# A hybrid decoder block on one core: pool order and alignment, and the order of loads at two stage borders

## The chip, the core and the metric

The kernel runs on one core of a Trainium2 chip. The metric is the device time of one execution in microseconds; the kernel before has a median of 2562.64 us over 3 runs (2560.47 to 2562.73). The profile is of one more execution, which took 2560.91 us.

## The reference

One decoder layer over 512 tokens of width 2048, all in float32, one batch, depth 1.

```
h   = RMSNorm(x)
[qA|kA|vA|qB|kB|vB|gA|gB] = h @ W_in              # 2048 x 8704
yA  = sliding-window attention (window 128, ALiBi, sinks; 16 query, 4 key heads of 64)
yB  = stick-breaking attention (16 heads of 64, strictly causal, no softmax)
x   = x + (sigmoid(gA) * (yA @ W_branch_a) + sigmoid(gB) * (yB @ W_branch_b)) @ W_out
x   = x + (silu(gate) * up) @ W_down,   [gate|up] = RMSNorm(x) @ W_ffn_in   # 5632 each
out = RMSNorm_final(x)
```

## The kernel before, in words

Every product is made at float32 accuracy from three matmuls: each operand is split into a high part and a low part, and high x high, high x low and low x high are summed in PSUM. A weight tile comes in through SP's queue as `raw`, ScalarE casts it to `whi` (L150), VectorE subtracts to get `wlo` (L151). `W.next()` hands these chunks out in the order of a plan and keeps up to three chunks ahead (`fill`, `split`).

The stages, in the order in which TensorE sees them (times from the trace):

1. 0 to about 850 us: input projection. `features` (L330 to L332) streams `fh`/`fl`, the split transposed activations, against stationary weights (128x512 matmuls); `tokens` (L346 to L348) has `fh`/`fl` stationary and streams 256 weight columns. Pieces of both attentions are queued with `later` and taken one at a time by `gap()` between products.
2. About 850 to 1040 us: gates and branch projections, `features` again, from about 890 us on with `yh`/`yl` as the streamed operand.
3. About 1040 to 1217 us: `rows` (L846 to L848), the product with W_out in four column blocks n, with `mh`/`ml` stationary. After each block the residual is added (L890), squares are summed (L854), the sum is stored to `x2_d`, and it is transposed and turned into forms (`turn_x1`, `make_forms`).
4. About 1217 to 2104 us: gate/up, 11 groups of 28 chunks. It is a seven-product block scheme (p1, p5, p6, p3, p7, p2, p4 in `ORDER`): the weight blocks are summed on VectorE (L224) and the activations enter as *forms*, seven tiles `fx` for each of 8 pairs of 128-wide slices. A chunk is 12 matmuls of 128x512 (`product`, L253 to L255): 6 with the form of an even pair stationary, 6 with that of an odd pair. Weight chunks are streamed.
5. About 2104 to 2546 us: the down projection in four parts of 3, 3, 3 and 2 quads, the same scheme twice for each part. The forms come back from DRAM through POOL's queue (`load_forms`, L999), and the block sums `x2` through SP's (L987). `into` (L1020) adds each finished product to `x2`. In the last part each token tile is squared, multiplied with the final gain and scaled (`finish`).

Memory. Left-hand pools: `cp` (constants), `wp` (raw, whi, wlo, three of each) and `tp` (47 general slots of 2 KB a partition: `yh`, `yl`, attention tiles, residual tiles, part of the forms). Right-hand pools grow down from byte 229,344 of a partition: first `ca` (constants of the attention, 10,240 bytes), below it `ep` (32 slots: `fh`, `fl`, later `mh`, `ml`). After stage 3 both are closed, and `fp` takes their place with `wx` (lowest), `fx` and `wz`. 229,344 is 32 past a multiple of 64; all sizes are multiples of 64, so each tile of `ca`, `ep` and `fp` starts 32 past a multiple of 64. In the built program each tile of `wp` and `tp` starts at a multiple of 64 (`raw` at 18,944, `tp` at 55,808). The right-hand tiles lie at 153,568 and above, the left-hand ones below 152,064.

Of the 8 pairs of gate/up forms, pairs 4 to 6 lie in `fp` (`form_slot`), the others in `tp`. Of the forms of a down part, even pairs lie in `fp`, odd ones in `tp`.

Order at the two borders. At the end of stage 3 the code adds the residual, flushes the queued pieces, transposes the last four slices, and only then closes `early` and opens `fp` (L903 on); a planned chunk of gate/up can't be loaded before `fp` exists, as its `wx` tile lies there. Then come the second norm's sum and four generators of forms (pairs 4 to 7): two forms of each at once, the other five in one piece each. At the end of stage 4 all 16 `x2` tiles take a slot and are issued on SP's queue; then `load_forms` takes the forms' slots. The last group's transposes and forms (`turn`, `forms`, stores to `form_d` at L973 through POOL's queue) are pieces that run during the first products of stage 5.

The slots of a pool are given out in program order, earliest released first, and an engine's instructions run in their order: an instruction that waits holds all that stand behind it on its engine or queue.

Of the kernel before, what the change touches and what calls it, by code (L numbers as in the profile page):

```python
# [45 lines left out]
def kernel(  # L46
# [64 lines left out]
    make_identity(nc, ident)  # L111
    ones = const("ones", P)
# [132 lines left out]
    def product(forms, banks, first, last):  # L245

        wh, wl, _ = W.next()
        for kk in range(2):
            a = forms[kk]
            for t in range(2):  # L250
# [7 lines left out]
    def group(nq, forms, after):  # L258
# [597 lines left out]
    def form_slot(p, name):  # L856
        if 4 <= p < 7:
            return fp.tile([P, T], F32R, tag="fx", name=uid("fx"), bufs=21)
        return slot("fx", F32R)

    def turn_x1(k, xr, tag):
# [15 lines left out]
        if k % 2 and k < KD // 2:  # L877
            forms_of(k // 2)
# [5 lines left out]
    for n in range(4):  # L884
# [3 lines left out]
        rows(KD, mh, ml, ob)  # L888
        for t in range(NT):
# [7 lines left out]
    while pieces:  # L897
        pieces.popleft()[1]()
# [4 lines left out]
    early.close()  # L903
    fp = ctx.enter_context(tc.tile_pool(name="fp", bufs=1, side="right", reuse_waits="tile"))
    inv2 = const("inv2", NT)
    nc.vector.tensor_reduce(out=inv2, in_=ss2.rearrange("p (t c) -> p t c", t=NT), axis=AX.X, op=ALU.add)
    rsqrt_mean(inv2, inv2, NT, [small(s, NT) for s in ("rv", "rr", "rq")])

    W.fill()
    late = [make_forms(xs2[2 * p], xs2[2 * p + 1], lambda name, p=p: form_slot(p, name)) for p in range(4, 8)]  # L910
# [73 lines left out]
    x2 = [[slot("x2") for _ in range(4)] for _ in range(NT)]  # L984
    for n in range(4):
        for t in range(NT):
            nc.sync.dma_start(out=x2[t][n], in_=x2_d[t][n])  # L987
    sst = const("sst", 4 * NT)
    gf = [None] * 4

    def load_forms(p0, np):
        res = [{} for _ in range(np)]
        for name in FORMS:
            for i in range(np):
# [4 lines left out]
                nc.gpsimd.dma_start(out=res[i][name], in_=form_d[p0 + i][name])  # L999
        return res  # L1000
# [13 lines left out]
    def down(nq, forms, n, last):  # L1014
        def into(half, col, op, done=False, end=False):
            def fn(b):
                for i in range(2):
# [23 lines left out]
            },  # L1041
        )
# [50 lines left out]
```

## Time and profile before

| | us |
|---|---|
| median of 3 runs | 2562.64 |
| profiled execution | 2560.91 |
| its span, first to last instruction | 2559.2 |
| TensorE matmul busy | 2512.7 (98%) |
| VectorE busy | 1981.0 (77%) |
| ScalarE busy | 1377.3 (54%) |
| GpSimd busy | 241.7 (9%) |
| moved by DMA | 407.99 MB, mean 159 GB/s |

Busy matmul time is a weak measure here: a matmul's record (about 0.39 us) overlaps the next one, which starts some 0.23 us later. So the pace is read from start to start in the timeline, and idle time from the note in brackets behind a row, which says how long the engine stood idle and what ended it.

### The profile page before, as it was taken

To read this page: it belongs to the slowest core of one execution; us is meant where nothing else is said; L and a number is where in the kernel's file an instruction comes from. 1 tells how busy PE (TensorE), PEld (TensorE's weight loads), DVE (VectorE), ACT (ScalarE), POOL (GpSimd) and SP (SyncE) were. 2 spreads that over 40 slices of the span, in tenths; PEclk is the share of its full clock that TensorE was granted. 3 is DMA by queue.
4 is the path that set the end of the run, shared out by engine and by line. 5 is a ranking of instruction groups with operands and counts; after the bars stand their busy time and mean duration, and the time that the engine had idled before them with its cause. 6 is when DMAs were issued, how large, how long until landed. Compare 5 with 4: busy or idle time off the path is not lost.

```text
span 2559.2 us, 33175 instructions
## 1 busy us (share of the span) xinstructions
PE 2512.7 (98%) x11529; PEld 2063.9 (81%) x11529; DVE 1981.0 (77%) x3457; ACT 1377.3 (54%) x2626; POOL 241.7 (9%) x465
## 2 busy tenths in 40 slices
PE   9999999999999999999899999999999999999998
PEld 8888878888887788888688888888888877888886
DVE  5688888888779644374888788887888877888888
ACT  6567777666657533364554555554555443333335
POOL 0000001111111000000010011100111122303000
PEclk9999999999999999999999999999999999999999
DMA  5232333333323644443456655556555689948552
GB/s 174 91 99 91 99 108 99 103 95 109 98 87 106 213 143 138 141 145 116 153 169 192 183 180 176 177 177 189 181 173 181 193 273 331 308 153 279 177 179 97
DMA packets 257319, 407.99 MB, mean 159 GB/s; under 512 B 16480, under 2 KB 103552, under 8 KB 257152
## 3 DMA queue, kind: packets, MB, share of 16 engines
q1 hardware_dynamic: 204400, 308.32, 38.7%
q0 software_dynamic: 45632, 84.96, 11.0%
q10 hardware_dynamic: 7120, 12.61, 1.3%
q8 instruction: 90, 1.47, 0.2%
q14 instruction: 77, 0.63, 0.1%
HBM read 344.48 MB, written 61.34 MB: 159 GB/s over the span
## 4 chain that ended last, share of the span: by engine, by line
PE 62%; issue 2%; DVE 1%; ACT 1%; DMA 1%; POOL 0%; ACTq 0%; POOLq 0%; DVEq 0%
PE mm L253 9%; PE mm L255 9%; PE mm L254 9%; PE at L253 7%; PE at L255 7%; PE at L254 7%; PE mm L331 3%; PE mm L330 3%; PE mm L332 3%; PE mm L848 1%; PE mm L847 1%; PE mm L846 1%; PE at L848 1%; PE at L847 1%; PE at L846 1%
## 5 line engine op out<-in xcount | busy, mean ns | idle before, releaser
L150 ACT CAST whi<-wx 128x1024 fp32r<-128x1024 f32 x264 | 277.3, 1051 | 331.4 <-PE mm L255 150.6
L254 PE MATMUL mm<-wlo,fx 128*128 128x512 f32 x1056 | 418.1, 396 | 0.2 <-DVE wlo L151 0.2
L255 PE MATMUL mm<-whi,fx 128*128 128x512 f32 x1056 | 417.0, 395 | 0.0
L151 DVE TENSOR_TENSOR wlo<-wx,whi 128x1024 fp32r<-128x1024 f32 x264 | 322.7, 1223 | 115.4 <-ACT whi L150 114.1
L151 DVE TENSOR_TENSOR wlo<-raw,whi 128x1024 fp32r<-128x1024 f32 (+1 forms) x201 | 244.1, 1215 | 191.6 <-ACT whi L150 189.6
L253 PE MATMUL mm<-whi,fx 128*128 128x512 f32 x1056 | 377.1, 397 | 13.3 <-ACT whi L150 9.5
L150 ACT CAST whi<-wz 128x1024 fp32r<-128x1024 f32 x198 | 208.0, 1050 | 288.4 <-PE mm L255 142.8
L332 PE MATMUL mm<-fh,wlo 128*128 128x512 f32 x896 | 356.0, 397 | 1.4 <-DVE wlo L151 1.4
L330 PE MATMUL mm<-fh,whi 128*128 128x512 f32 x896 | 355.7, 397 | 0.0
L331 PE MATMUL mm<-fl,whi 128*128 128x512 f32 x896 | 355.5, 397 | 0.0
L150 ACT CAST whi<-raw 128x1024 fp32r<-128x1024 f32 (+1 forms) x201 | 209.7, 1044 | 225.6 <-PE mm L331 142.1
L254 PE MATMUL at<-wlo,fx 128*128 128x512 f32 x792 | 311.6, 393 | 4.7 <-DVE wlo L151 4.7
L255 PE MATMUL at<-whi,fx 128*128 128x512 f32 x792 | 312.4, 394 | 0.0
L583 ACT COPY turned<-z 32x128 f32<-32x128 f32 (+3 forms) x888 | 242.5, 273 | 104.5 <-DVE z L743 57.6
L151 DVE TENSOR_TENSOR wlo<-wz,whi 128x1024 fp32r<-128x1024 f32 x198 | 240.6, 1222 | 53.6 <-ACT whi L150 53.4
L253 PE MATMUL at<-whi,fx 128*128 128x512 f32 x792 | 281.2, 395 | 0.5 <-ACT whi L150 0.5
L253 PEld LDWEIGHTS mm<-whi,fx 128*128 128x128 f32 x1056 | 198.6, 189 | 57.8 <-ACT whi L150 10.4
L254 PEld LDWEIGHTS mm<-wlo,fx 128*128 128x128 f32 x1056 | 199.9, 189 | 45.6 <-DVE wlo L151 1.3
L255 PEld LDWEIGHTS mm<-whi,fx 128*128 128x128 f32 x1056 | 199.7, 189 | 45.2
L332 PEld LDWEIGHTS mm<-fh,wlo 128*128 128x128 f32 x896 | 169.3, 189 | 42.9 <-DVE wlo L151 2.6
L331 PEld LDWEIGHTS mm<-fl,whi 128*128 128x128 f32 x896 | 169.3, 189 | 38.1
L330 PEld LDWEIGHTS mm<-fh,whi 128*128 128x128 f32 x896 | 169.4, 189 | 37.3
(252 smaller groups left out, 4166.5 us busy)
## 6 DMA issues: line engine op xcount, KB each, us to landing
raw<-in_w_in_dram SPq DMA_DIRECT2D x135, 512.0 KB, 3.6
raw<-in_w_ffn_in_dram SPq DMA_DIRECT2D x88, 512.0 KB, 3.7
wz<-in_w_ffn_in_dram SPq DMA_DIRECT2D x88, 512.0 KB, 4.4
wx<-in_w_ffn_in_dram SPq DMA_DIRECT2D x44, 512.0 KB, 4.5
raw<-in_w_ffn_down_dram SPq DMA_DIRECT2D x44, 512.0 KB, 4.8
wz<-in_w_ffn_down_dram SPq DMA_DIRECT2D x44, 512.0 KB, 5.4
raw<-in_w_out_dram SPq DMA_DIRECT2D x32, 512.0 KB, 3.7
wx<-in_w_ffn_down_dram SPq DMA_DIRECT2D x22, 512.0 KB, 4.8
```

The costliest lines, as they stand in the source:

```text
L150: nc.scalar.copy(hi[:, :n], raw[:, :n])
L151: nc.vector.tensor_tensor(out=lo[:, :n], in0=raw[:, :n], in1=f(hi[:, :n]), op=ALU.subtract)
L253: mm(banks[t], lhsT=hi, rhs=wh[:, kk, :], start=one, stop=False, skip_group_check=True)
L254: mm(banks[t], lhsT=hi, rhs=wl[:, kk, :], start=False, stop=False, skip_group_check=True)
L255: mm(banks[t], lhsT=lo, rhs=wh[:, kk, :], start=False, stop=end, skip_group_check=True)
L330: mm(b, lhsT=wh[:, kk, c], rhs=hi[k], start=(k == 0), stop=False)
L331: mm(b, lhsT=wh[:, kk, c], rhs=lo[k], start=False, stop=False)
L332: mm(b, lhsT=wl[:, kk, c], rhs=hi[k], start=False, stop=(k == nk - 1))
L583: copy(t4[c * Q : (c + 1) * Q, :, r], z4[r * Q : (r + 1) * Q, :, c])
L846: mm(banks[t], lhsT=hi[k][:, c], rhs=wh[:, kk, :], start=(k == 0), stop=False)
L847: mm(banks[t], lhsT=hi[k][:, c], rhs=wl[:, kk, :], start=False, stop=False)
L848: mm(banks[t], lhsT=lo[k][:, c], rhs=wh[:, kk, :], start=False, stop=(k == nk - 1))
```

## The change

- A pool `pad` of 24 floats (96 bytes) is opened first on the right-hand side, and `ep` is opened before `ca`. So `ep` starts under byte 229,248, a multiple of 64, and `ca` lies below it. One GpSimd memset writes the pad.
- Pieces are flushed, `early` is closed, `fp` is opened and `W.fill()` is called right behind the last block's matmuls, ahead of the residual additions. Forms of pair 4 are made with those of pairs 0 to 3, in `tp`; pairs 5 to 7 lie in `fp`. The late generators are three; after two forms of each at once, the next three are one form to a piece; the sum of the second norm is a piece behind them.
- The `x2` tiles go through POOL's queue, two token tiles at a time, in `load_forms` of the first part, ahead of the form whose product reads them first; those of columns n = 2, 3 come behind all forms.
- The last product p4 (two chunks) takes both chunks first and then runs by token tile: all matmuls of tile 0, its addition and `finish`, then tile 1.

```diff
     early = ctx.enter_context(ExitStack())
+    pad = ctx.enter_context(tc.tile_pool(name="pad", bufs=1, side="right"))
+    unused = pad.tile([P, 24], F32, tag="pad", name="pad")
+    ep = early.enter_context(tc.tile_pool(name="ep", bufs=32, side="right"))
     ca = early.enter_context(tc.tile_pool(name="ca", bufs=1, side="right"))
-    ep = early.enter_context(tc.tile_pool(name="ep", bufs=32, side="right"))
...
-    def product(forms, banks, first, last):
+    def product(forms, banks, first, last, chunk=None, tiles=(0, 1)):
-        wh, wl, _ = W.next()
+        wh, wl, _ = chunk or W.next()
...
+            if tail and name == "p4":
+                chunks = [W.next() for _ in range(nq)]
+                for t in range(2):
+                    for j in range(nq):
+                        product([forms[2 * j + i][name] for i in range(2)], u, False, j == nq - 1, chunks[j], (t,))
+                    after[name](u, (t,))
+                return
...
     def form_slot(p, name):
-        if 4 <= p < 7:
+        if p >= 5:
...
-        if k % 2 and k < KD // 2:
+        if k % 2 and k < KD // 2 + 2:
             forms_of(k // 2)
...
         rows(KD, mh, ml, ob)
+        if n == 3:
+            while pieces:
+                pieces.popleft()[1]()
+            early.close()
+            fp = ctx.enter_context(tc.tile_pool(name="fp", bufs=1, side="right", reuse_waits="tile"))
+            W.fill()
...
+    late = [make_forms(xs2[2 * p], xs2[2 * p + 1], lambda name, p=p: form_slot(p, name)) for p in (5, 6, 7)]
     for _ in range(2):
         for p, gen in enumerate(late):
-            xforms[4 + p] = next(gen)
+            xforms[5 + p] = next(gen)
+    for _ in range(3):
+        for gen in late:
+            later(lambda gen=gen: next(gen), 1)
     for gen in late:
         later(lambda gen=gen: [None for _ in gen], 1)
+    later(norm2, 1)
...
+    def load_x2(n, half):
+        for t in (2 * half, 2 * half + 1):
+            x2[t][n] = slot("x2")
+            nc.gpsimd.dma_start(out=x2[t][n], in_=x2_d[t][n])
+
+    FIRST_READ = {"p1": (0, 0), "p5": (1, 1), "p6": (1, 0), "p4": (0, 1)}
...
         for name in FORMS:
+            if p0 == 0 and name in FIRST_READ:
+                load_x2(*FIRST_READ[name])
```

## Rows read from the trace of the kernel before

**Rows 1.** The page: each engine's busy us, share of the span, instructions.

```profile
PE 2512.7 (98%) x11529; PEld 2063.9 (81%) x11529; DVE 1981.0 (77%) x3457; ACT 1377.3 (54%) x2626; POOL 241.7 (9%) x465
```

**Rows 2.** Busy us (instructions) of each engine in a stretch, clock, DMA share, GB/s.

```profile
2300.00:2400.00 100.00, 100.00 (x432) 80.84 (x431) 80.94 (x81) 37.65 (x37) 20.44 (x38) 1.00 0.76 236
```

**Rows 3.** TensorE's timeline: start us, length us; `fh` streamed, 25 starts apart.

```profile
250.01 0.40 PE L330 MATMUL mm<-fh,whi 128*128 128x512 f32 x1
...
255.84 0.40 PE L331 MATMUL mm<-fl,whi 128*128 128x512 f32 x1
```

**Rows 4.** TensorE's timeline, `yh` streamed, 27 starts apart.

```profile
1019.69 0.39 PE L332 MATMUL mm<-yh,wlo 128*128 128x512 f32 x1
...
1025.81 0.39 PE L332 MATMUL mm<-yh,wlo 128*128 128x512 f32 x1
```

**Rows 5.** TensorE's timeline in gate/up, p5: 16 starts with pairs 4 to 6, then 6 with pair 7.

```profile
1454.47 0.39 PE L254 MATMUL at<-wlo,fx 128*128 128x512 f32 x1
...
1458.20 0.40 PE L253 MATMUL at<-whi,fx 128*128 128x512 f32 x1
...
1459.59 0.62 PE L253 MATMUL mm<-whi,fx 128*128 128x512 f32 x2
```

**Rows 6.** TensorE's timeline, `mh`/`ml` stationary, 17 starts apart.

```profile
1213.29 0.39 PE L846 MATMUL at<-whi,mh 128*128 128x512 f32 x1
...
1217.25 0.39 PE L848 MATMUL at<-whi,ml 128*128 128x512 f32 x1
```

**Rows 7.** TensorE's timeline at the border to gate/up; in brackets idle us, who ended it.

```profile
1217.48 1.93 PE L107 MATMUL at<-ident,x 128*128 128x128 f32 x16
1224.83 1.22 PE L253 MATMUL mm<-whi,fx 128*128 128x512 f32 x2 [5.42 <-ACT whi L150]
...
1247.89 0.68 PE L254 MATMUL at<-wlo,fx 128*128 128x512 f32 x1 [3.32 <-DVE wlo L151]
```

**Rows 8.** Busy time by stretch around that border (columns as in rows 2).

```profile
1217.25:1251.64 34.39, 24.04 (x90) 17.75 (x88) 32.04 (x66) 22.95 (x50) 1.62 (x3) 0.85 0.64 214
1231.00:1248.00 17.00, 12.28 (x51) 8.83 (x51) 17.00 (x32) 9.26 (x18) 0.00 (x0) 1.00 0.41 126
1205.00:1215.00 10.00, 10.00 (x45) 8.03 (x44) 0.00 (x0) 0.00 (x0) 0.00 (x0) 1.00 0.12 45
```

**Rows 9.** SP's queue at that border: start us, length us, DMAs issued.

```profile
1217.44 2.54 SPq L217 DMA_DIRECT2D wx<-in_w_ffn_in_dram  x4
```

**Rows 10.** VectorE's timeline there: a chunk's low part, and two low parts of forms.

```profile
1246.62 1.22 DVE L151 TENSOR_TENSOR wlo<-wx,whi 128x1024 fp32r<-128x1024 f32 x1
...
1248.09 0.75 DVE L279 TENSOR_TENSOR fx<-turned,fx 128x256 fp32r<-128x256 f32 x2
```

**Rows 11.** TensorE's timeline at the border from gate/up to down.

```profile
2109.22 0.79 PE L253 MATMUL mm<-whi,fx 128*128 128x512 f32 x1 [3.79 <-DMA fx<-f1p]
...
2137.87 0.73 PE L253 MATMUL mm<-whi,fx 128*128 128x512 f32 x2 [4.05 <-ACT whi L150]
```

**Rows 12.** Busy time by stretch before and at that border (columns as in rows 2).

```profile
2105.16:2142.55 37.39, 29.03 (x111) 22.54 (x111) 23.99 (x36) 14.52 (x25) 13.50 (x26) 0.86 1.06 347
2030.00:2100.00 70.00, 70.00 (x311) 57.13 (x310) 57.54 (x69) 36.39 (x51) 17.61 (x33) 1.00 0.84 254
```

**Rows 13.** Timelines of POOL's queue, SP's queue and ScalarE at that border.

```profile
2102.64 0.54 POOL L999 DMA_DIRECT2D fx<-f1p  x1
...
2101.42 16.54 SPq L987 DMA_DIRECT2D x<-x  x16
...
2136.29 0.58 ACT L965 COPY e<-at 128x512 f32<-128x512 f32 x1 [8.14 <-DMA f20p<-fo]
```

**Rows 14.** The end: TensorE's last matmul, and ScalarE's last four scalings.

```profile
2546.33 0.40 PE L255 MATMUL mm<-whi,fx 128*128 128x512 f32 x1
...
2550.81 2.56 ACT L1009 ACTIVATE x<-x,inv 128x512 f32<-128x512 f32 x4 [0.69 <-DVE inv L360]
```

**Rows 15.** TensorE's longest wait in the attentions: us in total, times, longest.

```profile
PE at L648 <- ACT ph L588: 3.1, 1, 3.1
```

More of the change, by code (lines that the diff above doesn't have):

```diff
@@ L111 @@
     make_identity(nc, ident)
+    nc.gpsimd.memset(unused, 0.0)
     ones = const("ones", P)
@@ L243, in plan_group @@
             W.todo.append(lambda name=name, j=j: item(name, j))
-    def product(forms, banks, first, last):
-        wh, wl, _ = W.next()
+    def product(forms, banks, first, last, chunk=None, tiles=(0, 1)):
+        wh, wl, _ = chunk or W.next()
         for kk in range(2):
             a = forms[kk]
-            for t in range(2):
+            for t in tiles:
                 hi, lo = a[:, t * P : (t + 1) * P], a[:, (2 + t) * P : (3 + t) * P]
@@ L256, in product, with group @@
         gap()
-    def group(nq, forms, after):
+    def group(nq, forms, after, tail=False):
         u, c = [bank("mm") for _ in range(2)], None
         for name, j in steps(nq):
+            if tail and name == "p4":
[5 more added lines that the diff above has]
+                return
             if name in ("p5", "p2") and j == 0:
@@ L896, with norm2 @@
                 later(lambda k=k, xr=xr, tag=tag: turn_x1(k, xr, tag), 4)
-    while pieces:
-        pieces.popleft()[1]()
     for k in range(KD - 4, KD):
         turn_x1(k, xr, tag)
-    early.close()
-    fp = ctx.enter_context(tc.tile_pool(name="fp", bufs=1, side="right", reuse_waits="tile"))
     inv2 = const("inv2", NT)
[L906 to L910, printed above, removed]
+    def norm2():
+        nc.vector.tensor_reduce(out=inv2, in_=ss2.rearrange("p (t c) -> p t c", t=NT), axis=AX.X, op=ALU.add)
+        rsqrt_mean(inv2, inv2, NT, [small(s, NT) for s in ("rv", "rr", "rq")])
+    late = [make_forms(xs2[2 * p], xs2[2 * p + 1], lambda name, p=p: form_slot(p, name)) for p in (5, 6, 7)]
     for _ in range(2):
         for p, gen in enumerate(late):
-            xforms[4 + p] = next(gen)
+            xforms[5 + p] = next(gen)
+    for _ in range(3):
+        for gen in late:
+            later(lambda gen=gen: next(gen), 1)
     for gen in late:
         later(lambda gen=gen: [None for _ in gen], 1)
+    later(norm2, 1)
     form_d = [
@@ L981 @@
         gate_up(g)
[L984 to L987, printed above, removed]
+    x2 = [[None] * 4 for _ in range(NT)]
     sst = const("sst", 4 * NT)
     gf = [None] * 4
+    def load_x2(n, half):
[3 more added lines that the diff above has]
+    FIRST_READ = {"p1": (0, 0), "p5": (1, 1), "p6": (1, 0), "p4": (0, 1)}
     def load_forms(p0, np):
@@ L999, in load_forms @@
                 nc.gpsimd.dma_start(out=res[i][name], in_=form_d[p0 + i][name])
+        if p0 == 0:
+            for name in FIRST_READ:
+                n, half = FIRST_READ[name]
+                load_x2(n + 2, half)
         return res
@@ L1015, in into, with fn @@
         def into(half, col, op, done=False, end=False):
-            def fn(b):
-                for i in range(2):
+            def fn(b, tiles=(0, 1)):
+                for i in tiles:
                     t, m = 2 * half + i, n + col
@@ L1041, in down @@
             },
+            last and n == 2,
         )
```

## The prediction, made before the changed kernel was run

> **What bounds the kernel now.** I read the page's busy times first [rows 1]: TensorE has a matmul in flight for 98% of the span, VectorE is busy for 77%, ScalarE for 54%. So TensorE sets the end, and there are two ways to gain: the pace at which matmuls follow each other, and the stretches in which TensorE stands still. The tenths of the busy row hide both, so I went to the timeline from start to start, and then to the waits.
>
> Pace. With `yh` streamed, 27 starts take 6.12 us, 226.7 ns each [rows 4]; with `fh` streamed, 25 take 5.83 us, 233.2 ns [rows 3]: same line, same shape. With `mh` stationary 17 take 3.96 us, 232.9 ns [rows 6]. In gate/up, 16 starts whose stationary forms are of pairs 4 to 6 take 3.73 us, 233.1 ns, and the next six, of pair 7, 1.39 us, 231.7 ns [rows 5]. What the matmuls at 233 ns share is an operand in a right-hand pool, which starts 32 bytes past a multiple of 64. Pair 7 lies on the left; its six follow directly on shifted ones, as if the longer rhythm outlives its cause for some matmuls. In the down product, with right-hand and left-hand pairs in turn, 100 us hold 432 matmuls, 231.5 ns each [rows 2].
>
> Still. At the border to gate/up, 34.39 us hold 16 transposes (about 1.8 us) and 72 matmuls [rows 8]. At 226.7 ns these would take 18.1 us, so 16.3 us are lost: the wait of 5.42 us for the first cast weights and one of 3.32 us for VectorE [rows 7], smaller ones, and a granted clock of 0.85 on average, that is a mix of the two levels, 2.4 and 1.2 GHz, after the still stretches. At the border to down 37.39 us hold 111, of which 8 are transposes [rows 12]; 103 at 226.7 ns and 8 at 0.1 us make 24.1 us. The edges cut about one matmul, so some 13.4 us are lost: 3.79 us waiting for form f1p and 4.05 us for a cast [rows 11], and a clock of 0.86. Behind the last matmul there are some 6.7 us of work, until ScalarE's last scaling ends at 2553.4 [rows 14].
>
> **Alignment of the right-hand pools.** After the pad each right-hand tile starts at a multiple of 64, as the left-hand ones do, and I expect 226.7 ns everywhere. Counts come from the loops. Streamed `fh`/`fl`: 28 column blocks of features x 96 + 96 for the first one = 2784 matmuls, x 6.5 ns = 18.1 us. `rows`: 768 x 6.2 = 4.8 us. Gate/up: 77 products of 48, each with 18 matmuls on pairs 4 to 6 at 6.4 ns and 6 on pair 7 at 5.0 ns, 145 ns in all, 11.2 us. Down: 1848 x 4.8 = 8.9 us. Sum 43.0 us. The 960 matmuls of `tokens` stream 256 columns; no row here has an aligned one beside a shifted one, so they bring between nothing and the same 6.5 ns (6.2 us). I take nothing, since they stream from the aligned side and are half as long.
>
> This is not all kept. In the attentions VectorE and ScalarE run close behind TensorE, and once `ph` is 3.1 us late [rows 15]. If TensorE passes the last 60 us before such a point 3% faster, the same burst is 1.8 us later. I take 2.5 us off for all of them, with bounds of 0 and 10 us.
>
> The row shows a difference of 6.5 ns, which at 2.4 GHz is some 16 columns, 64 bytes of float32 [rows 3, 4]: one more piece of 64 bytes for an operand that straddles. The Trainium skill says in "SBUF — State Buffer", section "Specifications (TRN2)", that SBUF's lines are 16 bytes and that a crossing to a new line costs. By that rule a start 32 past a multiple of 64 is a line start like any other, and the alignment would bring 0 instead of 43 us. The rows do not decide between place and alignment; that is the first rival.
>
> **First weights early.** Before, `wx` is issued at 1217.44, when the last matmul that reads `ep` has begun [rows 6, 9]. After, the lowest 10,240 bytes of the new `fp`, the first two `wx` tiles and part of the third, lie where `ca` was, which nothing reads any more; the slot under the rest of the third is read early in the last block. So three loads can go while `rows` still runs: from 1205 to 1215 VectorE and ScalarE are idle and DMA has a share of 0.12 [rows 8]. Their casts and low parts have cover there too; gone is the wait of 5.42 us and the slow clock that follows it. What is late next is VectorE: it is busy 32.04 us of those 34.39, and all 17.00 us from 1231 to 1248 [rows 8]. At full pace six chunks and the transposes leave it 18.1 us. What leaves the stretch: three low parts at 1.22 = 3.7 us; pair 4's forms, some 12 operations at about 0.4 us, 4.5 us [rows 10], made in the block before, where it has room; and of the later five forms, four generators at once before (4 x 8 x 0.4 = 12.8 us), only about one form to a chunk after (3.6 us by then), 9.2 us. 32.0 - 17.4 = 14.6 us, which just fits. The added waits: 35 slots of `tp` now hold forms, with six or more turned slices, and an operation that takes a slot may wait for a residual tile's store on POOL's queue; behind it on VectorE stand the next chunk's sums. I keep 13 of the 16.3 us (bounds 5 and 16.3).
>
> **Sums and forms in order of use.** Before, 16 `x2` tiles take the earliest slots and 16.54 us of SP's queue, and f1p, needed first, is issued at 2102.64 [rows 13]. After, two `x2` tiles and then p1's forms take slots which the last group frees from its first products on. The 16 issues move to POOL's queue, at 0.54 us each 8.6 us there, and SP's weight loads no longer stand behind them. The stores of the last forms stand behind the loads on POOL's queue; ScalarE's copy waited 8.14 us for one of them [rows 13], which made the second still stretch. With most loads done by 2105, they go sooner. Against it: the bytes don't go away. 37 loads of 256 KB, 9.7 MB, move into 2030 to 2100, where 254 GB/s already go [rows 12]; over 70 us they would add 139 GB/s, while the busiest stretch here reached 347 GB/s at a share of 1.06. So some land late, and weights may be late with them. I keep 11 of 13.4 us (bounds 2 and 13.4).
>
> **Last product by tile.** Tile 0 of p4 is complete 2.7 us before the end, and behind the last matmul there is one tile's chain: one addition, square, gain and two scalings to an engine, against two tiles' interleaved. ScalarE's four scalings of 2.56 us [rows 14] would be two, 1.28 us, and a square of 0.8 us goes. But ScalarE still has the other half's four scalings when tile 0 comes, and two chains run one after the other could be 1.5 us longer. I take 1 us of gain (bounds +2.4 and -1.5). The pad's memset costs nothing: GpSimd is idle at the start.
>
> **Sum.** 43.0 - 2.5 + 13 + 11 + 1 = 65.5 us. The profiled execution took 2560.9 us, so 2495.4 us; the median of the runs is 1.7 us above it, so 2497 us.
>
> **The rivals.** First, the slow pace belongs to the high addresses and not to the start within 64 bytes: then the alignment brings nothing, 25 us remain, 2538 us. For it: each slow tile lies above byte 153,568, each fast one below 152,064. Against it: the excess is the time of one 64-byte piece for a streamed operand of 2 KB and for a stationary one of 512 bytes alike, and distance gives no such figure. Second, the pace is gained, but VectorE at the first border and DMA at the second give back most: the gain of 24 us falls to 6 and the attentions lose 5 us: 2562.6 - 44 = 2518 us. For it: 17.00 of 17 us [rows 8] and 1.06 [rows 12]. Third, slower: stores of forms get stuck on POOL's in-order queue. Place: the last group and the first part of down, where 14 to 28 stores are issued behind loads that wait for slots. Each stuck store holds a slot, then ScalarE, then TensorE, 4.05 us with some 2.4 us of slow clock behind it, 6.5 us. To be slower than before it must eat the other 54 us, so from 9 such stalls on; with ten 2573 us. Against it: before, with a worse order, there was one.
>
> **How the numbers follow.** My forecast 0.67, from 2485 (2562.6 - 43 - 16.3 - 13.4 - 2.4 = 2487.5 with nothing lost, and part of the 6.2 us of `tokens`) to 2508; first rival 0.13, second 0.16, third 0.04. The range of 2485 to 2522 us takes in forecast and second rival and leaves out the others. What a measurement can tell from no change here is 0.2%, 5 us; all cases but the third lie far beyond it: faster 0.95, same 0.01, slower 0.04.
>
> **What would show it.** Features with `fh`, `rows` and both stages of forms at 226.7 ns from start to start; if `fh` stays at 233 ns, the first rival holds. `wx` issued before 1205 in the old count, and no still stretch between the transposes and the first p1. f1p landed before the last group ends, ScalarE's copy without the wait of 8 us. A shorter chain behind the last matmul. I am wrong if the pace changes and the time does not, that is, if VectorE or DMA takes over for whole stages.

## The result, and the profile after

The kernel after takes 2548.46 us, the median of 4 runs (2547.38 to 2549.56), beside 2562.53 us for the kernel before on the same chip: a ratio of 0.9948, with a 95% interval of 0.9936 to 0.996. That is 14 us of the 65.5 that I forecast. The profiled execution took 2547.38 us, its span is 2545.4. The page's busy times hardly differ from [rows 1]:

```profile
PE 2502.8 (98%) x11529; PEld 2065.6 (81%) x11529; DVE 1980.7 (78%) x3457; ACT 1377.4 (54%) x2626; POOL 251.4 (10%) x482
```

**Pace.** TensorE's timeline of the kernel after, `fl` streamed, 24 starts apart (start us, length us):

```profile
250.10 0.39 PE L341 MATMUL mm<-fl,whi 128*128 128x512 f32 x1
...
255.68 0.39 PE L341 MATMUL mm<-fl,whi 128*128 128x512 f32 x1
```

5.58 us over 24 is 232.5 ns, against 233.2 [rows 3]; I had expected 226.7. Busy time by stretch of the kernel after says the same of the down product: 435 matmuls in 100 us, against 432 [rows 2]; the other two rows are the two borders, where the granted clock is now 0.90 and 0.91 against 0.85 and 0.86 [rows 8, 12].

```profile
1217.00:1252.00 35.00, 29.39 (x122) 23.40 (x121) 32.58 (x58) 24.61 (x46) 1.08 (x2) 0.90 0.57 192
...
2097.00:2134.00 37.00, 31.39 (x136) 25.23 (x135) 26.95 (x33) 13.41 (x17) 21.58 (x40) 0.91 1.02 344
...
2300.00:2400.00 100.00, 100.00 (x435) 81.64 (x434) 80.92 (x81) 37.77 (x36) 16.14 (x30) 1.00 0.72 230
```

**Border to gate/up.** TensorE's timeline of the kernel after:

```profile
1216.51 1.93 PE L109 MATMUL at<-ident,x 128*128 128x128 f32 x16
1223.54 1.22 PE L256 MATMUL mm<-whi,fx 128*128 128x512 f32 x2 [5.11 <-ACT whi L153]
```

The later stall of 3.32 us [rows 7] is gone, the first one (5.42 before) is not. SP did issue the first load at 1202.73 instead of 1217.44 [rows 9], so the cover was there. ScalarE's timeline shows what it did with it: nothing, for 14.31 us, and then squares, turned slices, a table load and the second norm's root before the first cast.

```profile
1215.34 0.63 ACT L864 ACTIVATE j<-x 128x512 f32<-128x512 f32 x1 [14.31 <-DVE x L906]
...
1218.31 2.42 ACT L885 ACTIVATE turned<-at,gcol 128x512 f32<-128x512 f32 x4
1220.75 1.28 ACT L366 ACT_TABLE_LOAD   x1
...
1222.45 1.04 ACT L153 CAST whi<-wx 128x1024 fp32r<-128x1024 f32 x1
```

SP's queue of the kernel after, four loads of `wx` as one row, and the longest wait of that queue between 1190 and 1235 us (us in total, times, longest). 13.4 of the 15.47 us are a wait of the second load for TensorE's last block (L858); it was issued at 1216.70, the first one at 1202.73:

```profile
1202.73 15.47 SPq L220 DMA_DIRECT2D wx<-in_w_ffn_in_dram  x4
...
SPq L220 <- PE at L858: 13.4, 1, 13.4
```

**Border to down.** TensorE's wait for f1p has grown from 3.79 [rows 11] to 5.49 us; the second stall of 4.05 us is gone. First TensorE's timeline, then POOL's queue. In the code the loads of even and odd pairs alternate, but an engine's order is set when the program is built, and it had put all even forms first: f1p stands right behind the last even form, which waits for the last product of gate/up:

```profile
2103.77 0.79 PE L256 MATMUL mm<-whi,fx 128*128 128x512 f32 x1 [5.49 <-DMA fx<-f1p]
```

```profile
2096.38 0.54 POOL L1022 DMA_DIRECT2D fx<-f4p  x1 [0.86 <-PE mm L258]
2096.91 1.09 POOL L1008 DMA_DIRECT2D x<-x  x2
2098.00 0.55 POOL L1022 DMA_DIRECT2D fx<-f1p  x1
```

**The end.** The last matmul, the output stores on SP's queue and ScalarE's last four scalings of the kernel after. From the last start to the span's end it is 14.55 us; before it was 12.87 (2559.2 - 2546.33 [rows 14]). The scalings end at 2538.67, 6.7 us before the span does: SP still issues stores, about 0.5 us each, until 2540.66, and the last one lands at 2543.81.

```profile
2530.85 0.40 PE L258 MATMUL mm<-whi,fx 128*128 128x512 f32 x1
...
2531.41 9.25 SPq L1039 DMA_DIRECT2D out_dram<-x  x16
...
2536.11 2.56 ACT L1036 ACTIVATE x<-x,inv 128x512 f32<-128x512 f32 x4 [0.29 <-DVE inv L370]
```

**Where the time is.** For each profiled execution I summed, over all pairs of successive matmul starts, what lies above full pace (226.67 ns for 512 columns, 113.4 for 256). A 512-column step under 262 ns counts as pace, a longer one, and the excess of all short shapes but 256 as well, as standing still or slow clock. What full pace is for those short shapes no row shows; it is taken alike in every column, so there the differences between columns count. "Border to down" includes the down stage, the attentions include the start. In us:

```
                            before  after  pad 56    before,  all
                                            (e5)  pad 56 (e6) (e17)
pace, 512 columns             44.6   39.8    5.0      5.3      5.4
pace, 256 columns              5.1    6.4    7.4      7.4      7.4
still: both attentions        21.2   21.3   27.0     27.4     27.0
still: border to gate/up      14.4    8.8    9.6     16.2      2.3
still: gate/up                 2.1    1.3    0.5      0.5      0.4
still: border to down         13.9    8.2    9.4     15.3      3.1
sum                          101.3   85.8   58.9     72.1     45.6
behind the last matmul        12.9   14.6   14.6     13.1     13.6
```

From before to after the sum falls by 15.5 and the end grows by 1.7: 13.8 us, as the spans do.

### The profile page after: what moved, and what is told of

It reads as the page before. It is cut to its first block, busy times and chain, and to the rows that moved or that the text cites. A ratio compares the mean times of both kernels' runs of the same rounds, so it can differ in the third digit from the quotient of the medians.

```text
span 2545.4 us, 33168 instructions
## 1 busy us (share of the span) xinstructions
PE 2502.8 (98%) x11529; PEld 2065.6 (81%) x11529; DVE 1980.7 (78%) x3457; ACT 1377.4 (54%) x2626; POOL 251.4 (10%) x482
## 4 chain that ended last, share of the span: by engine, by line
PE 63%; issue 2%; ACT 1%; POOL 0%; DVE 0%; DMA 0%; ACTq 0%; POOLq 0%; DVEq 0%
PE mm L256 9%; PE mm L258 9%; PE mm L257 9%; PE at L256 7%; PE at L258 7%; PE at L257 7%; PE mm L341 3%; PE mm L342 3%; PE mm L340 3%; PE mm L856 1%; PE mm L857 1%; PE mm L858 1%; PE at L856 1%; PE at L858 1%; PE at L857 1%
```

## The experiments

Ratios are to the kernel before, run on the same chip, with 95% intervals; the kernel after has 0.9948. The kernel before itself had medians from 2560.61 to 2562.53 us on these chips, so 1 to 2 us between runs on different chips show nothing.

**What sets the pace: a map (e1), and the alignment undone (e2).** e1 leaves out the whole block and runs only matmuls, in this manner (`a` is the place of the stationary operand, `b` that of the streamed one; other loops are cut):

```diff
+    for a in PL:
+        for b in PL:
+            for i in range(12):
+                mm(o(), lhsT=st(a, i), rhs=tiles[b][:, :T], start=True, stop=True)
...
```

> This kernel leaves out the whole block: it only runs 128x512 matmuls with fresh weights each, one operand at a fixed low place and the other one walking through 97 places of 2,112 bytes from byte 20,608 to 223,360 (first streamed, then stationary), then 8 x 8 places for both, then starts of 0 to 60 bytes past a multiple of 64, then 4 x 4 places while VectorE and ScalarE copy. Theory A (place): about 226.7 ns from start to start as long as both operands lie below about byte 152,064, about 232 ns when one lies above 153,472, in a step, whatever the start within 64 bytes and whether other engines work or not. Theory B (start within 64 bytes): 226.7 ns at every place, 233 ns at starts of 16 to 60 bytes. Theory C (two sides): 232 ns only where one operand lies high and the other low, 226.7 ns where both lie high. Theory D (the other engines' or DMA's traffic in the kernel makes the slow pace): 226.7 ns everywhere in the quiet part.

TensorE's timeline of e1 with the stationary operand at byte 62,848 (streamed tile first, then the stationary one; a single name means both; a row is 12 matmuls, so the distance to the next row's start, divided by 12, is the pace):

```profile
594.45 2.96 PE L78 MATMUL b<-at24k,at62k 128*128 128x512 f32 x12
597.25 2.91 PE L78 MATMUL b<-at62k 128*128 128x512 f32 x12
600.00 2.88 PE L78 MATMUL b<-at105k,at62k 128*128 128x512 f32 x12
602.72 2.88 PE L78 MATMUL b<-at147k,at62k 128*128 128x512 f32 x12
605.44 2.95 PE L78 MATMUL b<-at168k,at62k 128*128 128x512 f32 x12
608.23 2.90 PE L78 MATMUL b<-at181k,at62k 128*128 128x512 f32 x12
610.97 2.88 PE L78 MATMUL b<-at198k,at62k 128*128 128x512 f32 x12
613.68 2.96 PE L78 MATMUL b<-at221k,at62k 128*128 128x512 f32 x12
616.49 2.95 PE L78 MATMUL b<-at24k,at105k 128*128 128x512 f32 x12
```

The steps are 2.80, 2.75, 2.72, 2.72, 2.79, 2.74, 2.71 and 2.81 us: 232 to 234 ns for the tiles at 24,832, 168,448 and 221,248, and 226 to 229 ns for those at 62,848, 105,088, 147,328, 181,120 and 198,016. Height does not matter: 198k has the short step, 24k the long one. All tiles with the short step stand 128 past a multiple of 256, as the stationary operand does; 24k and 168k stand 0 past it, 221k 64. With the stationary operand at 24,832 it is the other way round: 24k and 168k at 227 to 228 ns, the 128s at 233. Over the 97 places the pace repeats every 4 tiles of 2,112 bytes, that is with the place within 256 bytes, up to 223,360 and without a step; only the first five places, whose matmuls were mixed with the opening ones, do not fit. In the last part only VectorE copied beside the matmuls, for some 26 of 44 us in each half; ScalarE's copies had run ahead, from 32 to 81 us, beside the first places of the walk, and those behind the fifth have the same pace as the later ones. Over the last six steps of each row, 8 of the 10 pairs with equal places ran at 226.7 ns (the others, 228.7 and 230.8, were still settling), the pairs with unequal ones at 232 to 233. Theories A to D all fell. Theory E took their place: **for starts at multiples of 64, the distance between streamed and stationary address, within 256 bytes, sets the pace.** Streamed 64 past the stationary one settled at 228.8 ns, 128 past it at 232.5 to 233.3, 192 past it at 233.3.

For other starts this does not hold, and e1 has them too: with the stationary operand 16 bytes ahead (144 and 128 past a multiple of 256) it ran at 233.3 ns, while e9 below has 226.7 for 16 and 0.

In these terms all left-hand tiles of the kernel start at multiples of 256 (18,944 and 55,808 are such), the right-hand ones before stood 224 past one (229,344 is 895 x 256 + 224), and the pad of 96 bytes moved them to 128 past it: aligned to 64, and as slow.

> The changed kernel without the pad, so that all right-hand tiles start 32 bytes past a multiple of 64 again. Theory A (place): the alignment is worth the 4.8 us by which the sum of starts fell between the two traces, so about 2553 us, ratio to before 0.996 to 0.997. Theory B (the start within 64 bytes, with the gain hidden by something else in the changed kernel): back to the slow rhythm and to 2562 us or more, ratio 1.000 or above.

2552.84 us, 0.9971 (0.9959 to 0.9982). Without the pad the 512-column pace loses 45.6 us instead of 39.8. So theory A's figure held (the alignment to 64 brought some 6 us), though its reason had fallen.

**Theory E in the kernel (e5 to e8).** Each is one number in one line, and all of them keep all tiles at multiples of 64. The first line added is e5's, the second e7's, the third e8's; e6 puts the pad of 56, with its memset, into the kernel before and changes nothing else there:

```diff
-    unused = pad.tile([P, 24], F32, tag="pad", name="pad")
+    unused = pad.tile([P, 56], F32, tag="pad", name="pad")
+    unused = pad.tile([P, 40], F32, tag="pad", name="pad")
+    unused = pad.tile([P, 8], F32, tag="pad", name="pad")
```

> The changed kernel with a pad of 56 floats (224 bytes) in place of 24, so that the right-hand tiles start at multiples of 256, as all left-hand ones do. Theory E (the pace depends on how far the streamed operand's address stands from the stationary one's within 256 bytes; equal ones run at 226.7 ns): all 512-column matmuls at 226.7 to 227 ns, the excess of 39.8 us over the kernel goes, perhaps 3 us more in tokens, some of it given back in the attentions: 2505 to 2511 us, ratio 0.978 to 0.981. Theory B (64 bytes are enough) or A (high addresses are slow): no change against the changed kernel, 2548 us, ratio 0.995.

2521.50 us, 0.9847 (0.9832 to 0.9862): 27 us less than after, not 38 to 43. TensorE's timeline of e5, `fh` streamed, 24 starts apart, 226.7 ns each:

```profile
249.95 0.39 PE L342 MATMUL mm<-fh,wlo 128*128 128x512 f32 x1
...
255.39 0.39 PE L342 MATMUL mm<-fh,wlo 128*128 128x512 f32 x1
```

And the busy time of e5 in a stretch of down, 443 matmuls against 435:

```profile
2300.00:2400.00 100.00, 100.00 (x443) 82.82 (x442) 84.86 (x85) 39.03 (x37) 13.93 (x26) 1.00 0.69 216
```

The pace came as theory E says, 34.8 of 39.8 us. What is missing was given back: 5.7 us in the attentions, 1.0 in the 256-column matmuls, 2.0 at the borders.

> The kernel before with nothing but a pad of 56 floats ahead of its right-hand pools, which then start at multiples of 256. Theory E: the excess of 44.6 us over the kernel goes, 2514 to 2521 us, ratio 0.982 to 0.985. Theory A: 2560 us, ratio 1.000. Theory B: some 43 us less as well, so this run alone does not part B from E; e5, e7 and e8 do.

2531.61 us, 0.9887 (0.9872 to 0.9902): the pad alone, with nothing else of the change, makes more than twice the change's gain. The range was missed for the same reason, 39.3 us of pace gained, 6.2 given back in the attentions, 2.3 in 256 columns, 3.2 at the borders.

> The changed kernel with a pad of 40 floats: right-hand tiles start 64 past a multiple of 256, left-hand ones at multiples of 256, all of them multiples of 64. Theory E, with the map's figures (streamed 64 past the stationary one: 228.4 ns; streamed 64 short of it: 233.6 ns): features with fh at about 228.4 ns instead of 232.7, so 12 us less, rows and the forms of gate/up and down in fp as slow as now or slightly slower: 2534 to 2539 us, ratio 0.990 to 0.992. Theories A and B: no change against the changed kernel, 2548 us, ratio 0.995.

2549.97 us, 0.9955 (0.9938 to 0.9971): a miss. The direction was right, the sizes not: stages that stream the right-hand tiles lost 11.6 us of pace against 16.8 in the kernel after (a gain of 5, not 12), those with right-hand stationary tiles 28.1 against 23.0. The two cancel. The same time as the kernel after is what theories A and B say, but not the two opposite changes. Features with `fh` and `fl` streamed ran at 230.6 ns here where the map has 228.8; why is open.

> The changed kernel with a pad of 8 floats: right-hand tiles start 192 past a multiple of 256, so 64 short of the next one, all of them multiples of 64. Theory E: the mirror image of the pad of 40 floats, features with fh at about 233.4 ns (2 us more than with the pad of 24), rows at about 228.4 ns (3 us less), gate/up and down with forms in fp near 228.4 ns (some 14 us less): 2530 to 2536 us, ratio 0.988 to 0.991. Theories A and B: no change against the changed kernel, 2548 us, ratio 0.995.

2534.96 us, 0.9898 (0.9884 to 0.9913), within theory E's range: 19.1 us against 16.8 in the streaming stages, 9.0 against 23.0 in the stationary ones. `rows` ran at 228.9 ns, the map's pace. By theories A and B e5, e7 and e8 would all be at 2548.

**A second map (e9)**, of distances in steps of 16, with operands in turn:

> Leaves out the whole block, like the first map; tiles of 2,112 bytes, the stationary one at byte 41,728, a multiple of 256. Stretches of 24 matmuls of 128x512: streamed operand 0 to 240 bytes past the stationary one in steps of 16 (and by 4, 8, 12, 244, 248, 252), then the stationary one past the streamed one by as much, then streams of 256 columns; then both kinds in turn, one by one, four by four and 64 by 64; last, both operands 64, 128 and 192 past a multiple of 256. Theory E: 226.7 ns at distance 0 and in all three cases where both stand equally far past a multiple of 256; 228 to 229 ns at 64, 232 to 234 ns at 128 and 192 and at most other distances. Rival F (only the streamed or only the stationary operand's own place within 256 bytes counts): both 64 or both 128 past a multiple of 256 run slowly, like one of them alone. Rival G (only multiples of 64 within 256 are of two kinds): all distances that are no multiple of 64 run alike at 233 ns.

TensorE's timeline of e9, 64 matmuls with the stationary tile at distance 0, 64 at distance 128, and again (from start to start 14.52 and 14.88 us, 226.9 and 232.5 ns):

```profile
398.00 14.69 PE L90 MATMUL b<-at109k,at41k 128*128 128x512 f32 x64
412.52 15.04 PE L90 MATMUL b<-at109k,at113k 128*128 128x512 f32 x64
427.40 14.68 PE L90 MATMUL b<-at109k,at41k 128*128 128x512 f32 x64
441.91 15.04 PE L90 MATMUL b<-at109k,at113k 128*128 128x512 f32 x64
```

Both operands 64, both 128 and both 192 past a multiple of 256 ran at 224 to 236 ns for the first six to ten matmuls and at 226 to 227 from there on, so rival F fell. With the stationary operand 16 or 240 bytes ahead, and with the streamed one 240 ahead, it settled at 226.7 too; from 64 to 224 (streamed one ahead) and from 32 to 224 (stationary one ahead) at 229 to 235, so rival G fell as well. Where starts are no multiples of 64 the same distance gave different paces: stationary one 4 bytes ahead, 226.7 ns with the places 0 and 252 (stationary, streamed), 232.4 with 4 and 0. So theory E holds for multiples of 64, as far as it was tested: with operands that keep their places within 256 bytes for a stretch. Between the multiples of 64 the places count as well, and by what rule is open.

The first stretch of e9 can't be read by distance: its four distances 0 to 48 are one tile, and its matmuls were mixed with the opening ones. The opening itself shows that what ran before counts. Its last 24 matmuls have the same operands in the same order in both maps, each pair at distance 0 but in other tiles than the pair before, mostly at another place within 256 bytes; they took 229.6 ns each in e1 (36.16 to 41.67 us) and 235.0 in e9 (36.48 to 42.12 us). What ends such a rhythm is open.

**First border (e3, e10, e13, e16).** Theory: the in-order queue of ScalarE held the first cast. e3 puts it first. `tc.issue_after(i)` queues what follows behind the instruction `i` of the same engine; `cast` holds the second chunk's cast (ScalarE) and low part (VectorE), and behind them stand the squares and the residual additions (cut):

```diff
-            W.fill()
+            before = len(W.made)
+            W.split()
+            W.split()
+            cast = W.made[before + 1]
+            behind.enter_context(tc.issue_after(cast[0]))
+            behind.enter_context(tc.issue_after(cast[1]))
...
+        with tc.issue_after(W.made[-1][0]), tc.issue_after(W.made[-1][1]):
+            norm2_now()
```

> The changed kernel with ScalarE's first two casts of gate/up weights and VectorE's two low parts queued ahead of the last block's squares and residual additions, and the second norm's sum, table load and root queued behind a later cast. Theory 1 (engine order: the weights had landed by 1207 us and only the in-order queue of ScalarE held the cast until 1222.45): the wait of 5.1 us before the first p1 goes and with it most of the half clock behind it, 5 to 8 us in all, so 2540 to 2543 us, ratio 0.991 to 0.993. Theory 2 (the weights land late, behind the last readers of the place): the wait stays, since the cast then waits for DMA, and the residual additions are late as well: 2548 us or more, ratio 0.995 or above.

2550.86 us, 0.9963 (0.995 to 0.9975): theory 2. (In e3 VectorE's block sums also stand behind the residual additions, and the third chunk behind the last turned slice.) ScalarE's timeline of e3:

```profile
1213.67 0.41 ACT L291 CAST fx<-turned 128x256 fp32r<-128x256 f32 x1 [12.66 <-PE at L860]
1213.98 1.04 ACT L154 CAST whi<-wx 128x1024 fp32r<-128x1024 f32 x1
1220.59 1.04 ACT L154 CAST whi<-wx 128x1024 fp32r<-128x1024 f32 x1 [5.57 <-DMA wx<-in_w_ffn_in_dram]
```

Only the first `wx` tile had landed early, at 1207.3; the second load waited for the last block here too and landed at 1220.5. Its tile does not lie where `ca` was (byte 165,760 in the built program, under an `mh` tile that the last block reads to its end; no row shows the byte, only the wait). e10 gives it another place, by two tags of two buffers in turn, with the pad of 56:

```diff
+                sub = ""
+                if tag == "wx":
+                    sub = turn_no[0] % 2
+                    turn_no[0] += 1
+                t = fp.tile([P, 1024], F32, tag=f"{tag}{sub}", name=uid(tag), bufs=2 if tag == "wx" else 4)
```

> The changed kernel with the pad of 56 floats, ScalarE's first two casts and VectorE's first two low parts of gate/up queued ahead of the last block's residual additions and squares, the second norm behind a later cast, and the wx tiles under two tags in turn, so that the second one lies over a slot that is read early in the last block. Theory 1 (the first p1 waited for ScalarE's order and for a second weight tile that had been given the place read last): the wait of 5.15 us before the first p1 goes with the half clock behind it, 6 to 8.5 us less than with the pad of 56 floats alone: 2513 to 2516 us, ratio 0.981 to 0.983. Theory 2 (VectorE and ScalarE have too much to do there, the wait moves to the third and fourth chunk): at most 3 us less, 2518 to 2522 us, ratio 0.983 to 0.985.

2520.34 us, 0.984 (0.9826 to 0.9853): in theory 2's range, but not for its reason. Three `wx` loads now landed by 1200.3. ScalarE's first row above shows the next cause, which e10 has too (12.32 us there): the cast of a form of pair 5, whose slot lies over `ep`, stands in front. e13 takes it away (`with tc.issue_after(last_turned[-1].ins)` around the first forms of pairs 5 to 7):

> As e10, and the first two forms of pairs 5 to 7 are queued on ScalarE behind the last turned slice. In e10 ScalarE stood idle for 12.32 us in front of the first weight cast, since the cast of a form of pair 5, whose slot lies over ep, stood before it and waited for the last block. Theory 1 (that one instruction held the casts until 1203.26): the two casts and low parts are done before 1203, the residual additions start on time, the transposes are followed by p1 with less than 1 us of wait; 6 to 8.5 us less than e5's 2521.5: 2513 to 2516 us, ratio 0.981 to 0.983. Theory 2 (the engines are full there): the wait moves to the third chunk, at most 3 us less than e5: 2518 us or more, ratio 0.983 or above.

2523.79 us, 0.9854 (0.984 to 0.9867): not faster. Both casts were done by 1201.1, but TensorE now ran two chunks of p1 ahead of the transposes, and the third cast, which my own edit had put behind the turned slices, came late. TensorE's timeline of e13:

```profile
1210.72 1.91 PE L109 MATMUL at<-ident,x 128*128 128x128 f32 x16
1215.31 0.73 PE L265 MATMUL mm<-whi,fx 128*128 128x512 f32 x2 [2.68 <-ACT whi L154]
```

e16 changes the point behind which they stand (`issue_after(cast[0])` in place of the last turned slice, three chunks at once by `W.fill()`):

> As e13, but on ScalarE the third cast and the first form of pair 5 stand directly behind the first two casts, ahead of squares and turned slices. Theory 1 (order only): no wait of more than 1 us between the last block and the fourth chunk of gate/up, and 4 to 8 us less than e5's 2521.5: 2513 to 2518 us, ratio 0.981 to 0.983. Theory 2 (the engines are full there): the wait comes back at the fourth or fifth chunk, 2520 us or more, ratio 0.984 or above.

2514.43 us, 0.9818 (0.9805 to 0.9831): theory 1, 7.1 us less than e5. In ScalarE's timeline of e16 the first three casts are made before the squares:

```profile
1196.39 1.05 ACT L154 CAST whi<-wx 128x1024 fp32r<-128x1024 f32 x1 [6.43 <-DMA wx<-in_w_ffn_in_dram]
1199.78 1.05 ACT L154 CAST whi<-wx 128x1024 fp32r<-128x1024 f32 x1 [2.34 <-PE at L867]
...
1205.22 1.06 ACT L154 CAST whi<-wx 128x1024 fp32r<-128x1024 f32 x1 [2.54 <-DVE x L920]
1206.18 0.63 ACT L873 ACTIVATE j<-x 128x512 f32<-128x512 f32 x1
```

TensorE's longest wait there is now 1.05 us, the loss of that border 2.0 us. The four steps (casts first, place of the second tile, form of pair 5, third cast) were taken on top of each other; what each is worth without the others is not shown.

**Second border (e4, e11, e14).** Theory: f1p's place in POOL's order, not its slot. e4 chains the loads in program order:

```diff
+    def pool_load(out, in_):
+        with tc.issue_after(prev[0].ins) if prev[0] else ExitStack():
+            prev[0] = nc.gpsimd.dma_start(out=out, in_=in_)
...
```

> The changed kernel with the loads of the first down part queued on POOL in the order of the program: form by form, each with its even and odd pairs and the block sums in front of it. Theory 1 (order on POOL: f1p stands behind f4p's last load, which waits for the last group's p4 until 2096.4 us, although its own slot is free long before): f1p lands before 2097 us, the wait of 5.49 us and the half clock behind it go, 5 to 8 us, so 2540 to 2543 us, ratio 0.991 to 0.993. Theory 2 (the slots of the odd pairs come free only with the last products): the wait stays at 5 us or grows, since the even pairs' loads now stand behind the odd ones too: 2548 us or more, ratio 0.995 or above.

2549.35 us, 0.9958 (0.9944 to 0.9972). Neither theory: f1p was issued at 2049.11, so its slot was free and the wait for it is gone, but the time is not. VectorE's and then TensorE's timeline of e4 show a new wait, for weights. The busy time by stretch has a DMA share of 1.11 (0.82 in the same stretch of the kernel after), and the last two rows, of e4 and then of the kernel after, have the same four loads of `wz` (KB each, median us from issue to landing): 8.4 us instead of 4.9. So the early loads made the weights late:

```profile
2069.51 1.23 DVE L227 TENSOR_TENSOR wx<-wx,wz 128x1024 f32<-128x1024 f32 x1 [6.30 <-DMA wz<-in_w_ffn_in_dram]
```

```profile
2071.93 0.50 PE L257 MATMUL mm<-wlo,fx 128*128 128x512 f32 x1 [3.57 <-DVE wlo L154]
```

```profile
2050.00:2070.00 20.00, 18.35 (x80) 14.68 (x79) 11.10 (x11) 6.73 (x8) 9.38 (x18) 1.00 1.11 367
```

```profile
wz<-in_w_ffn_in_dram SPq DMA_DIRECT2D x4, 512.0 KB, 8.4
wz<-in_w_ffn_in_dram SPq DMA_DIRECT2D x4, 512.0 KB, 4.9
```

e11 moves only the five loads that p1 needs, ahead of the even forms of p5, e14 the same five behind those of p7 (both with the pad of 56). The first line is e11's, the other two e14's; 0 stands for even pairs, 1 for odd ones:

```diff
+        names = [("p1", (0,)), ("p1", (1,))] + [(n, (0,)) for n in FORMS[1:]] + [(n, (1,)) for n in FORMS[1:]]
+        names = [(n, (0,)) for n in FORMS[:5]] + [("p1", (1,))]
+        names += [(n, (0,)) for n in FORMS[5:]] + [(n, (1,)) for n in FORMS[1:]]
```

> The changed kernel with the pad of 56 floats and, on POOL's queue, the two block sums and the three odd forms of p1 of the first down part ahead of the even forms of p5; all other odd forms and sums stay behind the last even one. Theory 1 (order on POOL): the wait of 5.47 us for f1p and the half clock behind it go without the waits for weights that all 37 early loads brought: 5 to 8 us less than with the pad alone, 2513 to 2517 us, ratio 0.981 to 0.983. Theory 2 (DMA has no room there at all, what is loaded earlier makes another load late): at most 3 us less, 2518 to 2522 us, ratio 0.983 to 0.985.

2518.63 us, 0.9832 (0.9818 to 0.9845), theory 2's range: the collision is smaller but there, in TensorE's timeline of e11:

```profile
2052.01 0.79 PE L257 MATMUL mm<-wlo,fx 128*128 128x512 f32 x1 [3.64 <-DVE wlo L154]
```

> As e11, with the five loads (two block sums, three odd forms of p1) queued behind the even forms of p7 instead of p1, that is at about 2064.5 us, where POOL stood idle for 8 us and DMA's share was 0.74 to 0.80 in e5 (0.94 to 1.05 where e11 had put them). Theory 1 (a collision of transfers): neither the wait of 5.47 us for f1p nor e11's wait of 3.8 us for weights; 5 to 8 us less than e5's 2521.5: 2513 to 2517 us, ratio 0.981 to 0.983. Theory 2 (no room at any time): a wait for weights of 3 us or more somewhere behind 2064, 2518 us or more, ratio 0.983 or above.

2515.15 us, 0.9818 (0.9805 to 0.9831), theory 1: 6.4 us less than e5. The five loads went out by 2061, somewhat earlier than I had meant; two waits for weights of 1.0 and 0.7 us remain, and the loss from there to the end is 4.5 us instead of 9.4.

**Together (e12, e15, e17).** e12 joins e10 and e11, e15 joins e13 and e14, e17 joins e16 and e14, all with the last product as before (`last and n == 2` replaced by `False`).

> Pad of 56 floats, casts first and p1's forms early together, and the last product as in the kernel before (both token tiles side by side). If both borders give what theory 1 says of each: 2521.5 less 6 to 8.5, less 5 to 8, less 1.7 us for the end (behind the last matmul's start 14.55 us in the changed kernel and 12.87 us before): 2503 to 2509 us, ratio 0.977 to 0.980. If the borders only pass their waits on: 2514 to 2520 us, ratio 0.982 to 0.984.

2515.50 us, 0.9822 (0.9809 to 0.9835): the second range, as e10 and e11 alone had brought little.

> Pad of 56 floats, e13's order at the first border, e14's at the second, and the last product as in the kernel before. If theory 1 holds at both: 2521.5 less 6 to 8.5, less 5 to 8, less about 1.2 us for the end: 2503 to 2510 us, ratio 0.977 to 0.980. If theory 2 holds at both: about 2515 us as e12, ratio 0.982.

2515.32 us, 0.9818 (0.9804 to 0.9831): theory 2's figure. What it has is e14's gain; e13 had brought none.

> Pad of 56 floats, e16's order at the first border, e14's at the second, and the last product as in the kernel before. Theory 1: e14's 2515.2 less 4 to 8, less about 1.2 us for the end: 2506 to 2510 us, ratio 0.978 to 0.980. Theory 2: 2514 us or more, ratio 0.9815 or above.

2506.08 us, 0.9783 (0.977 to 0.9797), theory 1. In all three joined kernels the parts add up: by the parts' own times, and 1 us for the end, e12 should be at 2516.5, e15 at 2516.4 and e17 at 2507.1, and each is about 1 us below. So neither border passes its gain on to the other, and what a border brings alone it brings joined. e17 is 42 us below the kernel after. The page of e17, and its two borders by stretch, at a granted clock of 1.00 (159 and 168 matmuls in 35 and 37 us, 122 and 136 in the kernel after):

```profile
PE 2467.2 (99%) x11529; PEld 2059.8 (82%) x11529; DVE 1978.6 (79%) x3457; ACT 1378.8 (55%) x2626; POOL 252.0 (10%) x482
```

```profile
1195.00:1230.00 35.00, 34.55 (x159) 27.89 (x157) 27.32 (x41) 20.24 (x37) 2.16 (x4) 1.00 0.55 200
2065.00:2102.00 37.00, 36.43 (x168) 29.79 (x167) 33.55 (x36) 17.11 (x21) 19.55 (x36) 1.00 1.07 360
```

## Why the prediction was wrong, point by point

- **The step that failed: "After the pad each right-hand tile starts at a multiple of 64, as the left-hand ones do, and I expect 226.7 ns everywhere."** It was to bring 43.0 us and brought 4.8. The count behind it was sound: with the distance at 0 the kernel before loses 39.3 us of pace less (e6). What was wrong is the unit, and that I looked at one operand's own address. In the trace of before all right-hand tiles had the same place within 256 bytes, so no row of it could tell 64 from 256, or place from distance; a pad of 56 floats would have been right by both readings.
- **The argument of 16 columns or 64 bytes** fell: aligned to 64 and 128 past the other operand, the matmuls ran as slowly (232.5 ns). No run shows that the 6.5 ns are the time of one piece of 64 bytes. The Trainium skill's "SBUF — State Buffer", section "Specifications (TRN2)", which I weighed there, speaks of 16-byte lines; as I read it, a start at any multiple of 16 is a line's start and would cost nothing. On the multiple of 32 it was nearer to the result than I was, but e9 has 229 to 235 ns at most distances that are multiples of 16, where that reading makes no difference.
- **The first rival** was nearest in time (2538) and partly right in what it said of the pad, but not in its reason: no height in e1 is slow by itself. Its price was 10 us too low, because it kept my terms for the borders.
- **The other rivals.** The second needed the pace, which came only in e5; there the attentions gave back 5.7 us, close to its 5. Of the third's stuck queue one case came, with a load (f1p, 5.49 us) and not a store.
- **Attentions**: I took off 2.5 us, with 0 and 10 as bounds. In the kernel after nothing was given back (21.2 and 21.3), as nothing was gained; where the pace came, 5.7 to 6.2 us (e5, e6).
- **tokens**: taken as nothing, bounds 0 and 6.2. It went the other way, 1.3 us worse in the kernel after and 2.3 worse at distance 0.
- **Border to gate/up**: 13 forecast, 5.6 measured (14.4 to 8.8). The early issue was right for one load of three. Two things were not read: which slot the second tile gets, and what stands in front of the cast on ScalarE. VectorE, which I took for the limit, was none: e16 loses 2.0 us at that border where the kernel before lost 14.4, with VectorE's work reordered and no less of it.
- **Border to down**: 11 forecast, 5.7 measured (13.9 to 8.2). The second stall went, as I said; the first grew, since I had p1's forms in "slots which the last group frees from its first products on". The slots were free (e4), but the odd forms stood behind the even ones on POOL's queue. My doubt about DMA's room was right: e4 shows it, and e11 has the same wait for weights.
- **The end**: 1 us of gain forecast, 1.7 us lost. The two chains run one after the other, the possibility that I had priced at 1.5. With the old order e17 has 13.6 us there, e16 with the new one 14.55. My chain also ended at the last scaling; the stores behind it, some 6 us in both kernels, were not in it.
- By terms: 4.8 - 1.3 - 0.1 + 5.6 + 0.8 + 5.7 - 1.7 = 13.8 us.

## What to carry to other kernels

Compare the start addresses of what a matmul streams and of what it holds, both within 256 bytes, before anything else: here that was one pad and 30 us. A load that is issued early is worth nothing until you have read which slot it gets and what stands in front of its consumer on an in-order engine. Each wait that is taken away shows the next one, so a step is only proven by the time, not by the wait that is gone.

## What the runs showed of the hardware that was not expected

- The pace of 128x512 float32 matmuls with fresh weights depends, for starts at multiples of 64, on the distance between streamed and stationary address within 256 bytes: 226.7 ns at 0, 228.8 to 229 with the streamed one 64 ahead, 232 to 234 at 128 and 192, anywhere from byte 20,608 to 223,360 (e1, e9). Between the multiples of 64 it ran at 226.7 to 240 ns, and the places count as well as the distance. In the kernel the best pace was run with all tiles at multiples of 256 (e5, e6).
- After a change of operands the pace takes up to ten matmuls to settle, and with two kinds in turn, four by four, it never does: a mean of 231 to 232 ns (e9).
- Streams of 256 columns have another best distance: 120.0 ns at 0, 113.3 with the streamed one 112 or 192 bytes ahead (e9). e7, where `tokens` has its streamed operand 192 ahead, lost 4.1 us there instead of e5's 7.4, where 113.3 would lose none. A placement for both shapes was not tried.
- With a DMA share of 1.11 loads of 512 KB took 8.4 us to land instead of 4.9, and VectorE waited 6.30 us for one (e4).
